# Down projection of four SwiGLU layers woven into their gate and up projection, nine 512-row pairs by seven products

## The chip, the cores and the metric

The kernel runs on one core of a Trainium2 chip. The metric is the device time of one execution in microseconds (us), lower is better; a measurement is a median of several executions, and the profile shows one execution with every instruction of the five engines: TensorE (PE, with its weight loads as PEld), VectorE (DVE), ScalarE (ACT), GpSimd (POOL) and SyncE (SP, which here only issues DMAs).

## The reference

Two layers of an encoder work on 256 tokens of width 1024, all in float32. Each layer has a half-step feed-forward block (below "FFN"), an attention block ("mix") and a second FFN:

```python
def swiglu(x, w_gate, w_up, w_down):
    return (jax.nn.silu(x @ w_gate) * (x @ w_up)) @ w_down

for l in range(DEPTH):
    x = x + 0.5 * swiglu(rms_norm(x, ffn1_norm[l]), ffn1_w_gate[l], ffn1_w_up[l], ffn1_w_down[l])
    ...
    x = x + merged @ w_out[l]
    x = x + 0.5 * swiglu(rms_norm(x, ffn2_norm[l]), ffn2_w_gate[l], ffn2_w_up[l], ffn2_w_down[l])
```

The inner width D_FF is 2816. Only the four FFNs and the way in which one block hands x to the next bear on this change; the attention is left as it is.

## The kernel before, in words

**Precision.** A float32 operand is split into a high part (rounded to the fast matmul type, on ScalarE) and a low part (the rest, on VectorE: `split_to`, L192 to L194). One product of two split operands is three matmuls, hi by hi, hi by lo, lo by hi (`three`, L176 to L179). So every weight tile of 128x1024 costs a DMA, one ACTIVATE and one TENSOR_TENSOR before TensorE can use it. The tiles come from rings: `raw` with 4 buffers, `wh` and `wl` with 6 each.

**One FFN** (`ffn`, L317) takes the inner width in 11 chunks of 256. For each chunk TensorE multiplies both token halves (t = 0 and 1, 128 tokens each) with the gate and up columns: `project`, 8 products of 128x512 for each half, 48 matmuls for a chunk. `glu` (L457) makes silu(gate) * up, `send` (L328) lays it out as 16-bit halves and starts a DMA transpose, and `arrive` (L337) puts the transposed chunk together and splits it. When all 11 chunks are through, `down` (L399) runs the down projection alone.

**The plan of the down projection** is a string of one letter for each chunk, `PLAN = "SFGFGGFGGSS"`. A chunk is two token halves by two 128-row blocks, against two rows by two column halves of w_down: eight products of blocks in the plain way ("S", `out_rows`). The other eight chunks use a seven-product scheme of fast 2x2 matrix multiplication: sums and differences of the four blocks of each side (`arrive` L348 to L350 for the activations, `differences` L366 for the weights), seven products "1" to "7" (`sevens`, L384), and at the end sums of the products (`combine`, L431). Here "1" means the block in the corner. Three of the eight chunks have their weight differences made ahead, during gate and up (`prepare`, PREP and PREP_FIRST), and read the rows of w_down once more for the rest.

**The end of a stage.** The last chunks are plain; after each group of products for a token half t and a column half d, VectorE adds the group to x (L311), and `norm` (L202) for the next stage is deferred by four products: TensorE transposes four blocks of x (L210), VectorE scales them by the gain (L217), ScalarE and VectorE split them, ScalarE sums the squares. The last FFN stores x instead.

**What sets the order.** The order of TensorE is that of the program. VectorE, ScalarE and SyncE are ordered by a scheduler; inside a tied chain (`linked`, L124, and `chain`) each instruction is made to follow the one before it on its engine in program order. Before the change only the opening of the first FFN is tied. All engines work through their own queues in order.

Of the kernel before, what the change touches and what calls it, by code (L numbers as in the profile page):

```python
# [2 lines left out]

# [12 lines left out]
U16 = mybir.dt.uint16  # L16
# [35 lines left out]
PLAN = "SFGFGGFGGSS"  # L52
PREP = {3: 1, 5: 3, 7: 6}
PREP_FIRST = {5: 1, 7: 3, 8: 6}
NS = sum(kind != "S" for kind in PLAN)
# [3 lines left out]
def hybrid_encoder(ctx, tc, x, w_gu1, w_d1, w_in, b_gate, qk_gain, rpb, sink, t5,  # L59
# [73 lines left out]
    def parts(r, nk=2, n=512):  # L133
        wh = ring.tile([P, 2, 512], F32R, name="wh", tag="wh", bufs=RING)
        wl = ring.tile([P, 2, 512], F32R, name="wl", tag="wl", bufs=RING)
        split_to(wh[:, :nk, :n], wl[:, :nk, :n], r)
        return wh, wl

    def load(src, nk, n):
        raw = ring.tile([P, 2, 512], F32, name="raw", tag="raw", bufs=RAW)  # L140
        r = raw[:, :nk, :n]
        nc.sync.dma_start(r, src)
        return parts(r, nk, n)
# [5 lines left out]
    def piece(w, l, i, c0, n, nk=KD // 2):  # L149
        at = (nk * c0 + i * n) * 2 * P  # L150
        return load(w[l, at:at + 2 * P * n].rearrange("(p k n) -> p k n", p=P, k=2), 2, n)
# [4 lines left out]
    def rows(w, l, k):  # L156
        return load(w[l, k * P:(k + 1) * P, :].rearrange("p (h n) -> p h n", h=2), 2, 512)
# [32 lines left out]
    last_hi = [None]  # L190

    def split_to(hi, lo, src):  # L192
        last_hi[0] = linked("act", lambda: nc.scalar.activation(hi, src, AF.Copy))  # L193
        linked("dve", lambda: nc.vector.tensor_tensor(lo, src, hi.bitcast(F32), ALU.subtract))  # L194
# [7 lines left out]
    def norm(t, n, half, apart=False):  # L202
# [9 lines left out]
        if apart and half == 1:  # L212
            for i in range(4):
                linked("act", lambda: nc.scalar.activation(xg[:, i, :], tp[:, i, :], AF.Copy,
                                                           scale=gain[:, n, 4 + i:5 + i]))
        else:
            linked("dve", lambda: nc.vector.tensor_tensor(  # L217
                xg, tp, gain[:, n, ks].unsqueeze(2).to_broadcast([P, 4, P]), ALU.mult))
        split_to(*(x[:, ks, :] for x in xT[t]), xg)
        if not apart:  # L220
            square(t, half)

# [73 lines left out]
    def out_rows(get, acc, k0, k1, last, w, l, scale, after, rest=None, split=None):  # L296
        pieces = [(k, *rows(w, l, k)) for k in range(k0, k1)]
        if split:
            split()
        for t in range(T):  # L300
            for d in range(2):
                for k, wh, wl in pieces:
                    first = acc[t][d] is None
                    if first:
                        acc[t][d] = out_bank(t, d)
                    xh, xl = get(t, k)
                    three(acc[t][d], xh, xl, wh[:, d, :], wl[:, d, :], first, last and k == k1 - 1)
                    tick(1)
                if last:
                    xd = xs[t][:, d * 512:(d + 1) * 512]  # L310
                    updated = nc.vector.scalar_tensor_tensor(xd, acc[t][d], scale, xd, op0=ALU.mult, op1=ALU.add)  # L311
                    if rest and t + d == 0:
                        with tc.issue_after(updated.ins):
                            rest()
                    after(t, d)

    def ffn(l, n, w_gu, w_d, after):  # L317
        with tc.tile_pool(name="ffn", bufs=1) as fp:
            hs = {}
            SLOT = ((1, 2), (0, 3))  # L320

            on_way, apart = [], {}

            def half(c, p, shape=None, dtype=F32R):
                m, n = (4, NFC - NS) if PLAN[c] == "S" else (7, NS)
                return fp.tile(shape or [P, m, P], dtype, name=p if shape else f"{p}{m}", tag=f"{p[:2]}{m}", bufs=n)

            def send(c, hh):  # L328
                m = 8 if PLAN[c] == "S" else 14
                z = half(c, "lo16", [P, m, P], U16)[:, :8, :].rearrange("p s n -> p (s n)")  # L330
                apart[c] = nc.scalar.activation(z.rearrange("p (two n) -> p two n", two=2),  # L331
                                                hh.bitcast(U16).rearrange("p s (n two) -> p two (s n)", two=2), AF.Copy)
                zT = half(c, "hi16", [P, m, P], U16)[:, :8, :]
                nc.sync.dma_start_transpose(zT, z)
                on_way.append((c, zT))

            def arrive():  # L337
                c, zT = on_way.pop(0)
                if PLAN[c] == "S":
                    a = fp.tile([P, 4, P], F32, name="a4", tag="a4")  # L340
                else:
                    a = fp.tile([P, 8, P], F32, name="a", tag="sums", bufs=2)
                joined = nc.scalar.activation(a[:, :4, :].bitcast(U16).rearrange("p s (n two) -> p two (s n)", two=2),  # L343
                                              zT.rearrange("p (two s) n -> p two (s n)", two=2), AF.Copy)
                behind(joined, apart[c + 1] if c + 1 < NFC else last_hi[0])
                hi, lo = half(c, "hi"), half(c, "lo")
                if PLAN[c] != "S":
                    for to, x, y, op in ((4, 0, 3, ALU.add), (6, 1, 0, ALU.subtract), (5, 4, 1, ALU.subtract),  # L348
                                         (7, 2, 5, ALU.subtract)):
                        nc.vector.tensor_tensor(a[:, to, :], a[:, x, :], a[:, y, :], op)  # L350
                    split_to(hi, lo, a[:, 1:, :])
                else:
                    split_to(hi, lo, a)
                hs[c] = (hi, lo)

            def get(t, k):
                return [h[:, SLOT[t][k % 2], :] for h in hs[k // 2]]

            stored = {}

            def block_row(k, c0=0, n=2):
                r = ring.tile([P, 2, 512], F32, name="raw", tag="raw", bufs=RAW)[:, :n, :]
                nc.sync.dma_start(r, w_d[l, k * P:(k + 1) * P, :n * 512].rearrange("p (h n) -> p h n", h=n))
                return r

            def differences(r0, r1, into):  # L366
                sub = lambda to, x, y: nc.vector.tensor_tensor(to, x, y, ALU.subtract)  # L367
                u = fp.tile([P, 2, 512], F32, name="u", tag="sums", bufs=2)
                sub(u[:, 0, :], r1[:, 1, :], r0[:, 1, :])
                sub(u[:, 1, :], r0[:, 1, :], r0[:, 0, :])  # L370
                us = into("u", u)
                v = fp.tile([P, 2, 512], F32, name="v", tag="sums", bufs=2)
                sub(v[:, 0, :], r1[:, 1, :], u[:, 1, :])
                sub(v[:, 1, :], r1[:, 0, :], v[:, 0, :])
                return us, into("v", v)

            def prepare(c):
                def into(name, r):
                    hl = [fp.tile([P, 2, 512], F32R, name=f"{name}{p}{c}", tag=f"{name}{p}{c}") for p in "hl"]
                    split_to(*hl, r)  # L380
                    return hl
                stored[c] = differences(block_row(2 * c), block_row(2 * c + 1), into)

            def sevens(c):  # L384
                r0 = block_row(2 * c, n=1 if c in stored else 2)
                r1 = block_row(2 * c + 1)
                place = ("xh0", "xl0", "xh1", "xl1")[(c - PLAN[:c].count("S")) % 4]
                both = act.tile([P, 2, 512], F32R, name="corner", tag=place)
                corner = [both[:, i, :] for i in range(2)]
                split_to(*corner, r0[:, 0, :])  # L390
                low = parts(r1)
                us, vs = stored.get(c) or differences(r0, r1, lambda name, r: parts(r))
                if on_way and c >= 5:
                    arrive()
                half = lambda pair, i: [p[:, i, :] for p in pair]
                return (("1", 0, corner), ("2", 1, half(low, 0)), ("3", 6, half(low, 1)), ("5", 3, half(us, 1)),
                        ("6", 4, half(vs, 0)), ("4", 2, half(vs, 1)), ("7", 5, half(us, 0)))

            def down():  # L399
                acc = [[None] * 2 for _ in range(T)]  # L400
                banks = {"2": (0, 0), "3": (0, 1), "4": (1, 0)}
                extra, rest = {}, []
                c = 0
                while c < NFC:
                    if PLAN[c] == "S":
# [460 lines left out]
```

## Time and profile before

| | |
|---|---|
| median of 3 runs | 1063.62 us (1062.95 to 1063.72) |
| the profiled execution | 1063.93 us, of which 1062.1 us are the span from its first to its last instruction |
| instructions | PE 4949, DVE 1337, ACT 1070, POOL 118 |
| first transposes of each next stage (L210) | 183.37, 352.74, 528.95, 706.16, 875.32 us |
| last matmul | 1057.83 us |
| data moved | 224.15 MB, mean 211 GB/s |

Split at those places, the span is six stages: FFN, mix, FFN, FFN, mix, FFN. The view of engine busy time by stretch shows them, with the columns: stretch, its length, busy time and instructions of PE, PEld, DVE, ACT and POOL, the granted TensorE clock, the share of DMA time, GB/s.

```profile
15.00:190.00 175.00, 172.22 (x752) 139.27 (x751) 146.88 (x203) 125.95 (x153) 17.80 (x27) 1.00 0.77 226
190.00:366.00 176.00, 175.84 (x936) 148.96 (x934) 146.11 (x269) 123.93 (x237) 48.67 (x40) 1.00 0.60 186
366.00:543.00 177.00, 176.91 (x787) 146.13 (x787) 150.22 (x204) 127.64 (x153) 1.11 (x2) 1.00 0.79 226
543.00:717.00 174.00, 173.23 (x771) 142.92 (x771) 146.93 (x201) 124.29 (x150) 1.10 (x2) 1.00 0.75 223
```

TensorE is busy nearly all of the time in every stage, VectorE for five sixths of it, ScalarE for seven tenths. The profile models the end of a matmul, so a stop of TensorE shows in full only from the start of one matmul to the start of the next.

### The profile page before, as it was taken

To read this page: it belongs to the slowest core of one execution; us is meant where nothing else is said; L and a number is where in the kernel's file an instruction comes from. 1 tells how busy PE (TensorE), PEld (TensorE's weight loads), DVE (VectorE), ACT (ScalarE), POOL (GpSimd) and SP (SyncE) were. 2 spreads that over 40 slices of the span, in tenths; PEclk is the share of its full clock that TensorE was granted. 3 is DMA by queue.
4 is the path that set the end of the run, shared out by engine and by line. 5 is a ranking of instruction groups with operands and counts; after the bars stand their busy time and mean duration, and the time that the engine had idled before them with its cause. 6 is when DMAs were issued, how large, how long until landed. Compare 5 with 4: busy or idle time off the path is not lost.

```text
span 1062.1 us, 14462 instructions
## 1 busy us (share of the span) xinstructions
PE 1052.2 (99%) x4949; PEld 871.4 (82%) x4949; DVE 878.6 (83%) x1337; ACT 747.6 (70%) x1070; POOL 118.6 (11%) x118
## 2 busy tenths in 40 slices
PE   9999999999999999999999999999999999999998
PEld 6888787888888888888888888878888888887886
DVE  6678899889886759879977887998898866788897
ACT  6777765788773667886567886757887646687772
POOL 1000040244420000000000000003534100000000
PEclk9999999999999999999999999999999999999999
DMA  7979866665655489996758997657566555798862
GB/s 247 262 225 254 253 207 200 204 193 176 194 182 159 159 231 259 258 252 196 228 171 224 275 262 202 214 160 249 174 198 177 189 159 189 214 277 227 240 201 99
DMA packets 112522, 224.15 MB, mean 211 GB/s; under 512 B 54032, under 2 KB 60208, under 8 KB 112448
## 3 DMA queue, kind: packets, MB, share of 16 engines
q1 hardware_dynamic: 112256, 223.14, 70.6%
q8 instruction: 39, 0.64, 0.2%
q0 software_dynamic: 192, 0.08, 0.1%
q14 instruction: 35, 0.29, 0.1%
HBM read 210.59 MB, written 1.06 MB: 199 GB/s over the span
## 4 chain that ended last, share of the span: by engine, by line
PE 76%; DVE 11%; DMA 6%; ACT 4%; issue 3%; SPq 0%; POOL 0%; ACTq 0%; DVEq 0%; POOLq 0%
PE g L177 18%; PE g L179 18%; PE g L178 18%; DVE wl L194 6%; DMA raw<-in_w_gu 4%; PE acc L177 4%; PE acc L179 4%; PE acc L178 4%; ACT wh L193 2%; DMA raw<-in_w_d 1%; PE sc L584 1%; PE po L619 1%; PE pt L605 1%; PE g L242 1%; ACT a L343 1%
## 5 line engine op out<-in xcount | busy, mean ns | idle before, releaser
L194 DVE TENSOR_TENSOR wl<-raw,wh 128x1024 fp32r<-128x1024 f32 x336 | 405.4, 1218 | 63.2 <-ACT wh L193 60.2
L193 ACT ACTIVATE wh<-raw 128x1024 fp32r<-128x1024 f32 x336 | 345.5, 1043 | 95.8 <-DMA raw<-in_w_gu 43.4
L177 PE MATMUL g<-wh,xh 128*128 128x512 f32 (+1 forms) x976 | 382.0, 391 | 0.6 <-DVE hh L463 0.3
L178 PE MATMUL g<-wl,xh 128*128 128x512 f32 (+1 forms) x976 | 377.7, 387 | 0.7 <-DVE wl L194 0.7
L179 PE MATMUL g<-wh,xl 128*128 128x512 f32 (+1 forms) x976 | 377.6, 387 | 0.1
L179 PEld LDWEIGHTS g<-wh,xl 128*128 128x128 f32 x976 | 183.4, 188 | 38.7 <-DVE xl L194 1.1
L177 PEld LDWEIGHTS g<-wh,xh 128*128 128x128 f32 x976 | 183.6, 188 | 35.9 <-DVE hh L463 2.4
L178 PEld LDWEIGHTS g<-wl,xh 128*128 128x128 f32 x976 | 183.7, 188 | 35.3 <-DVE wl L194 2.1
L178 PE MATMUL acc<-wl,hi 128*128 128x512 f32 x180 | 70.2, 390 | 1.3 <-DVE wl L194 1.3
L177 PE MATMUL acc<-wh,hi 128*128 128x512 f32 x180 | 70.8, 393 | 0.0
L179 PE MATMUL acc<-wh,lo 128*128 128x512 f32 x180 | 70.2, 390 | 0.0
L183 POOL TENSOR_TENSOR rs_y<-ms,mhalf 128x1 f32<-128x1 f32 x12 | 7.7, 644 | 542.6 <-DVE ms L231 533.8
L343 ACT ACTIVATE a<-hi 128x1024 uint16<-128x1024 uint16 x44 | 59.5, 1353 | 0.0
L463 DVE SCALAR_TENSOR_TENSOR hh<-g,rs_y,hh 128x256 f32<-128x256 f32 x88 | 42.1, 478 | 17.9 <-ACT hh L462 17.8
L331 ACT ACTIVATE lo<-hh 128x1024 uint16<-128x1024 uint16 x44 | 46.3, 1051 | 14.8 <-DVE hh L463 14.7
L462 ACT ACTIVATE hh<-g,rs_y 128x256 f32<-128x256 f32 x88 | 40.5, 461 | 22.2 <-PE g L179 21.7
L350 DVE TENSOR_TENSOR a<-a 128x128 f32<-128x128 f32 x128 | 31.9, 287 | 29.3 <-ACT a L343 28.6
L194 DVE TENSOR_TENSOR lo<-a,hi 128x896 fp32r<-128x896 f32 (+1 forms) x44 | 43.0, 977 | 11.1 <-ACT hi L193 11.1
L367 DVE TENSOR_TENSOR u<-raw 128x512 f32<-128x512 f32 x64 | 41.9, 684 | 11.8 <-DMA raw<-in_w_d 11.6
L597 POOL TENSOR_TENSOR S<-S,sm 128x512 f32<-128x512 f32 x32 | 37.1, 1159 | 65.5 <-DVE sm L596 34.6
L193 ACT ACTIVATE hi<-a 128x896 fp32r<-128x896 f32 (+1 forms) x44 | 37.7, 857 | 8.3 <-DVE a L350 7.8
L193 ACT ACTIVATE corner<-raw 128x512 fp32r<-128x512 f32 x32 | 20.0, 626 | 30.9 <-DMA raw<-in_w_d 26.0
(186 smaller groups left out, 1508.0 us busy)
## 6 DMA issues: line engine op xcount, KB each, us to landing
raw<-in_w_gu SPq DMA_DIRECT2D x176, 512.0 KB, 4.5
raw<-in_w_d SPq DMA_DIRECT2D x100, 512.0 KB, 4.3
raw<-in_w_in SPq DMA_DIRECT2D x64, 512.0 KB, 4.2
raw<-in_w_out SPq DMA_DIRECT2D x16, 512.0 KB, 3.5
bb<-in_b_gate SPq DMA_DIRECT2D x16, 256.0 KB, 3.4
raw<-in_w_bsw SPq DMA_DIRECT2D x8, 512.0 KB, 3.9
raw<-in_w_bna SPq DMA_DIRECT2D x8, 512.0 KB, 3.5
raw<-in_w_d SPq DMA_DIRECT2D x12, 256.0 KB, 2.7
```

Of the source, the lines that this page charges most:

```text
L177: nc.tensor.matmul(ps, xh, wh, start=first, stop=False)
L178: nc.tensor.matmul(ps, xh, wl, start=False, stop=False)
L179: nc.tensor.matmul(ps, xl, wh, start=False, stop=last)
L193: last_hi[0] = linked("act", lambda: nc.scalar.activation(hi, src, AF.Copy))
L194: linked("dve", lambda: nc.vector.tensor_tensor(lo, src, hi.bitcast(F32), ALU.subtract))
L331: apart[c] = nc.scalar.activation(z.rearrange("p (two n) -> p two n", two=2), hh.bitcast(U16).rearrange("p s (n two) -> p two (s n)", two= ...
L343: joined = nc.scalar.activation(a[:, :4, :].bitcast(U16).rearrange("p s (n two) -> p two (s n)", two=2), zT.rearrange("p (two s) n -> p tw ...
L350: nc.vector.tensor_tensor(a[:, to, :], a[:, x, :], a[:, y, :], op)
L367: sub = lambda to, x, y: nc.vector.tensor_tensor(to, x, y, ALU.subtract)
L462: linked("act", lambda: nc.scalar.activation(h, gate, AF.Silu, scale=rstd[t]))
L463: linked("dve", lambda: nc.vector.scalar_tensor_tensor(h, up, rstd[t], h, op0=ALU.mult, op1=ALU.mult))
L597: nc.gpsimd.tensor_tensor(S_, S_, sm.unsqueeze(2).to_broadcast([P, T, S]), ALU.mult)
```

## The change

The plan string, `prepare` and the separate phase `down` go. The first chunks of an FFN (three in the first FFN of the kernel, two in the others) run gate and up alone. From then on each pass of the loop does gate and up of chunk c and, behind it, six of the seven products of pair q = c - first_quad ("562374"); the seventh, "1", is kept for the end, with its operands in `one` and `corner`. Eight pairs (first FFN) or nine (the others) go by seven products, three or two chunks in the plain way at the end, with four column groups `plain`. The weight differences are made for each pair in the same pass from two rows of w_down held in a tile of their own (`rows`). From the second half of chunk first_quad - 1 on, all work of VectorE and ScalarE in an FFN is tied in program order. The stage end (`closing`) is tied too, also that of the attention block: each `norm` stands behind the next group of products, and two or three weight tiles of the next stage are loaded and split between its steps.

```diff
-PLAN = "SFGFGGFGGSS"
-PREP = {3: 1, 5: 3, 7: 6}
+HELD = 3
+SECOND_LAG = 4.0
+MIX_EARLY = 2
...
+    def start_split(hi, lo, src):
+        linked("act", lambda: nc.scalar.activation(hi, src, AF.Copy))
+        return lambda: linked("dve", lambda: nc.vector.tensor_tensor(lo, src, hi.bitcast(F32), ALU.subtract))
...
+    def closing(plain, n, early, between=lambda: None):
+        more = iter(early)
+        ahead = lambda: next(more, lambda: None)()
+        ahead()
+        plain(0, 1)
+        steps = norm_steps(0, n + 1, 0)
+        next(steps)
+        between()
+        next(steps)
+        plain(1, 0)
+        more_steps = norm_steps(0, n + 1, 1)
+        next(more_steps)
+        next(steps, None)
+        ahead()
+        next(more_steps)
+        plain(1, 1)
+        steps = norm_steps(1, n + 1, 0)
...
+        defer(SECOND_LAG, ("norm", 1, 1), lambda: norm(1, n + 1, 1))
+        chain.clear()
...
+            def quad(q, got):
+                for name in "562374":
+                    product(name, [h[:, SLOT[name], :] for h in hs[q]], got[name], q == QUADS - 1 and name in "567")
...
+            def down_end(rest, start):
+                p6, u = [act.tile([P, 512], F32, name=name, tag="xg", bufs=2) for name in ("p6", "ends")]
+                linked("act", lambda: nc.scalar.activation(p6, acc["6"], AF.Copy, scale=0.5))
...
+                for j in range(QUADS):
+                    product("1", [one[j][:, i, :] for i in range(2)], [corner[j][:, i, :] for i in range(2)],
+                            j == QUADS - 1)
...
+                plain(0, 0, "2")
+                if after:
...
+                closing(lambda t, d: plain(t, d, {(0, 1): "3", (1, 0): "4", (1, 1): "8"}[t, d]), n, early,
+                        lambda: linked("dve", lambda: nc.vector.tensor_tensor(x1, x1, twice(u), ALU.add)))
...
+                for j, (t, i) in enumerate(order):
+                    steps(ps, t, i, tiles[i])
+                    if j == 1:
+                        uv = sums(q)
+                        tile, low = start(c, 3)
+                        low()
+                        tiles.append(tile)
+                    elif j == 3:
+                        got.update(block("56", uv[:, :2, :]))
+                        got.update(block("23", rows_of[q][:, 2:, :]))
+                    elif j == 5:
+                        rest = arrive()
+                        got.update(block("74", uv[:, 2:, :]))
+                        rest()
+                        keep_corner(q)
+                ahead_tiles = []
+                tile, low = start(c + 1, 0)
+                ahead_tiles.append(tile)
+                steps(ps, 0, 3, tiles[3])
+                glu(0, ps[0], pair)
+                low()
+                tile, low = start(c + 1, 1)
+                ahead_tiles.append(tile)
+                steps(ps, 1, 3, tiles[3])
+                glu(1, ps[1], pair)
+                low()
+                tile, low = start(c + 1, 2)
+                ahead_tiles.append(tile)
+                send(c, pair[0])
+                low()
+                quad(q, got)
```

`steps(ps, t, i, tile)` is two products of gate and up for token half t; `sums` makes the four weight differences of a pair in three instructions, `block` splits two of them, `keep_corner` the corner block, `start` fetches a weight tile and starts its split. In `arrive` the corner block of the activations is split by itself (128x128) and the other six blocks in one go (128x768, before 128x896).

How this moves the instructions is seen on VectorE. The first place is the middle of the second FFN. Before, between one chunk's `glu` and the next, the rows are these (`wl` are low parts of gate and up weights, `u` and `v` weight differences made ahead, `a` the block sums of the activations, `hh` the glu):

```order
L463 SCALAR_TENSOR_TENSOR hh<-g,rs_y,hh 128x256
L194 TENSOR_TENSOR wl<-raw,wh 128x1024
L367 TENSOR_TENSOR v<-raw,u 128x512
L194 TENSOR_TENSOR wl<-raw,wh 128x1024
L367 TENSOR_TENSOR v<-raw,v 128x512
L194 TENSOR_TENSOR wl<-raw,wh 128x1024
L463 SCALAR_TENSOR_TENSOR hh<-g,rs_y,hh 128x2x128
```

Behind this stretch the same mixture goes on, and nothing of the products of a pair stands in it. In the changed kernel a pass of the same FFN reads, from the weight differences (`uv`, from the two `rows` of w_down) to the first `glu` and the low part behind it (`one` and `corner` are the operands of product "1"):

```order
L413 TENSOR_TENSOR uv<-rows 128x2x512
L413 TENSOR_TENSOR uv<-rows,uv 128x512 x2
L208 TENSOR_TENSOR wl<-raw,wh 128x1024
L208 TENSOR_TENSOR wl<-uv,wh 128x1024
L208 TENSOR_TENSOR wl<-rows,wh 128x1024
L208 TENSOR_TENSOR one_4089<-a,one_4089 128x128
L396 TENSOR_TENSOR a<-a 128x128 x4
L208 TENSOR_TENSOR wl<-uv,wh 128x1024
L208 TENSOR_TENSOR lo<-a,hi 128x768
L208 TENSOR_TENSOR corner_4104<-rows,corner_4104 128x512
L497 SCALAR_TENSOR_TENSOR hh<-g,rs_y,hh 128x256
L208 TENSOR_TENSOR wl<-raw,wh 128x1024
```

The second `hh` and two more `wl<-raw` close the pass. The work on a pair of w_down now stands inside the pass, in one fixed place, and three of the four `wl` of the next chunk stand around the two `hh`.

The second place is the end of the third FFN, VectorE again. Before, from the first addition of product sums to the second transposed half (`p` and `ends` are the sums of products, `x_80` and `x_81` the token halves of x, `acc` a plain group, `xg` the scaled transposed x):

```order
L437 SCALAR_TENSOR_TENSOR p_6725<-tp,p_6724 128x512 x2
L194 TENSOR_TENSOR wl<-raw,wh 128x1024
L311 SCALAR_TENSOR_TENSOR x_80<-acc,x_80 128x512
L437 SCALAR_TENSOR_TENSOR ends<-tp,p_6725 128x512
L442 TENSOR_TENSOR x_81<-x_81,p_6725 128x512
L442 TENSOR_TENSOR x_80<-x_80,p_6725 128x512
L442 TENSOR_TENSOR x_81<-x_81,ends 128x512
L217 TENSOR_TENSOR xg<-tp,x_80 128x512
```

Four instructions on product sums stand here between a plain group (`acc`) and the scaling of its transposes. In the changed kernel the same stretch (`m` are product sums, each in its own bank):

```order
L471 TENSOR_TENSOR x_80<-x_80,ends 128x512
L442 SCALAR_TENSOR_TENSOR x_80<-m_5599,x_80 128x512
L208 TENSOR_TENSOR wl<-raw,wh 128x1024
L442 SCALAR_TENSOR_TENSOR x_80<-m_5603,x_80 128x512
L234 TENSOR_TENSOR xg<-tp,x_80 128x512
L489 TENSOR_TENSOR x_81<-x_81,ends 128x1024
L208 TENSOR_TENSOR xl_6775<-xg,xh_6774 128x512
L442 SCALAR_TENSOR_TENSOR x_81<-m_5611,x_81 128x512
```

The additions for x_81 that stood between a group and its transposes are gone from there or stand behind them, and one weight tile of the next stage (`wl`) stands between the first group and the second.

More of the change, by code (lines that the diff above doesn't have):

```diff
@@ L317, in ffn @@
-    def ffn(l, n, w_gu, w_d, after):
-        with tc.tile_pool(name="ffn", bufs=1) as fp:
[L319 to L326, printed above, removed]
-            def send(c, hh):
[L329 to L333, printed above, removed]
+    def closing(plain, n, early, between=lambda: None):
[15 more added lines that the diff above has]
+        steps = norm_steps(1, n + 1, 0)
+        next(steps)
+        next(more_steps, None)
+        ahead()
+        next(steps)
+        next(steps, None)
+        defer(SECOND_LAG, ("norm", 1, 1), lambda: norm(1, n + 1, 1))
+        chain.clear()
@@ L338, in arrive @@
                 c, zT = on_way.pop(0)
[L339 to L397, printed above, removed]
@@ new lines, in ffn, with product @@
+            acc, used = {}, {}
+            def product(name, x, w, last):
+                if name not in acc:
+                    pool, tag, m = BANK[name]
+                    acc[name] = pool.tile([P, 512], F32, name=f"m{name}", tag=tag, bufs=m)
+                used[name] = used.get(name, 0) + 1
+                three(acc[name], *x, *w, used[name] == 1, last)
+                tick(1)
+            def quad(q, got):
+                for name in "562374":
+                    product(name, [h[:, SLOT[name], :] for h in hs[q]], got[name], q == QUADS - 1 and name in "567")
@@ L469, in ffn @@
                     both, second = opening(w_gu, l, lambda ps: glu(0, ps, pair))
-                elif n == 0 and c == 1:
-                    pieces = second
-                else:
-                    pieces = columns(w_gu, l, c * 512, 512)
-                if c >= 2:
-                    arrive()
-                prep = PREP if n else PREP_FIRST
-                if c in prep:
-                    prepare(prep[c])
-                for t in range(T):
-                    if not first:
-                        glu(t, project(t, pieces, 512), pair)
-                    elif t:
-                        glu(t, both[t], pair)
@@ new lines, in ffn @@
+                if c == first_quad - 1:
+                    fetch_rows(0)
+                    chain["act"], chain["dve"] = glu(0, project(0, pieces, 512), pair)
+                    tiles = []
+                    for i in range(3):
+                        tile, low = start(c + 1, i)
+                        low()
+                        tiles.append(tile)
+                    rest = arrive()
+                    glu(1, project(1, pieces, 512), pair)
+                    rest()
+                    send(c, pair[0])
+                    continue
@@ L488, in hybrid_encoder @@
+                send(c, pair[0])
+                low()
+                quad(q, got)
+                tiles = ahead_tiles
+            tile, low = start(NFC, 3)
+            low()
+            tiles.append(tile)
+            down_end(tiles, start)
+            chain.clear()
     vec_d = dram.tile([NH, 511], F32, name="vec_d")
```

289 lines of the change are left out of this document (190 added, 99 removed).

## The prediction

> **What bounds the kernel now.** I began with the busy times of the page:
>
> ```profile
> PE 1052.2 (99%) x4949; PEld 871.4 (82%) x4949; DVE 878.6 (83%) x1337; ACT 747.6 (70%) x1070; POOL 118.6 (11%) x118
> ```
>
> TensorE looks full, but the end of a matmul is modelled, so I asked the timeline of TensorE for the steps from start to start (columns: start, duration, instruction, idle before and what ended it). The first two rows have 13 matmuls between them, left out here:
>
> ```profile
> 107.63 0.39 PE L178 MATMUL g<-wl,xh 128*128 128x512 f32 x1
> ...
> 110.80 0.39 PE L177 MATMUL g<-wh,xh 128*128 128x512 f32 x1
> 111.39 0.50 PE L178 MATMUL g<-wl,xh 128*128 128x512 f32 x1 [0.20 <-DVE wl L194]
> 111.73 0.40 PE L179 MATMUL g<-wh,xl 128*128 128x512 f32 x1
> 111.96 0.39 PE L177 MATMUL g<-wh,xh 128*128 128x512 f32 x1
> ```
>
> Undisturbed, a 128x512 matmul takes (110.80 - 107.63) / 14 = 0.2264 us. The stop in the fourth row shows how a wait reads: the view says 0.20 us idle, but the step is 111.39 - 110.80 = 0.59, so 0.36 us are lost (0.20 plus 0.39 - 0.23 that the modelled end hides), and the next step, 0.34, loses 0.11 more. A wait of a matmul thus costs its idle time plus 0.27 us, one of a transpose its idle time plus 0.16.
>
> The Trainium skill ("Perfetto Trace Analysis", Identifying the Most-Contended Engine) holds matmul busy time a bad measure and goes by weight loads instead, 82% here. By it some 190 us would be left to win; but in the trace a stretch without a stop has the same share, so I read 82% as the full rate. That is this row of the busy times by stretch (PE, PEld, DVE, ACT, POOL busy, granted clock, DMA share, GB/s):
>
> ```profile
> 400.00:420.00 20.00, 20.00 (x90) 16.58 (x89) 17.77 (x27) 15.98 (x19) 0.00 (x0) 1.00 0.96 260
> ```
>
> 16.58 of 20 us are weight loads, TensorE never stops, and the clock is granted in full. So only two things can shorten this kernel: fewer matmuls, and the stops. All stops of TensorE that the waits view lists behind the opening are these (waiter, releaser: total idle us, times, longest):
>
> ```profile
> PE tp L210 <- DVE x L311: 1.5, 4, 0.6
> PE acc L178 <- DVE wl L194: 1.3, 1, 1.3
> PE g L178 <- DVE wl L194: 0.7, 2, 0.5
> PE g L177 <- DVE hh L463: 0.3, 1, 0.3
> PE pt L605 <- POOL S L597: 0.2, 1, 0.2
> ```
>
> **The change, part by part.**
>
> *Matmuls.* The plan string has eight seven-product letters and three plain ones, 8 x 7 + 3 x 8 = 80 products. Three of the four FFNs now have nine and two: 9 x 7 + 2 x 8 = 79. That is 3 products of 3 matmuls: 9 x 0.2264 = **2.0 us** on the path, since TensorE is the path.
>
> *Stops that go.* The first four rows above lie in or at the ends of FFNs, in code that is replaced: 1.5 + 1.3 + 0.7 + 0.3 = 3.8 us idle, plus 4 x 0.27 for the matmuls and 4 x 0.16 for the transposes, 5.5 us. Stops shorter than the modelled end show no idle time; two larger ones are
>
> ```profile
> 125.49 0.39 PE L179 MATMUL g<-wh,xl 128*128 128x512 f32 x1
> 125.98 0.50 PE L177 MATMUL g<-wh,xh 128*128 128x512 f32 x1
> ...
> 975.82 0.39 PE L179 MATMUL g<-wh,xl 128*128 128x512 f32 x1
> 976.32 0.50 PE L177 MATMUL g<-wh,xh 128*128 128x512 f32 x1
> ```
>
> of 0.49 and 0.50 us a step, so 0.26 + 0.27 lost and 0.11 twice behind them, 0.8 us. Together **6.3 us**. The row `pt` is in the attention and stays.
>
> *Does VectorE keep up in the woven pass?* TensorE needs 48 + 18 = 66 matmuls, 66 x 0.2264 = 14.94 us. For VectorE I take steps from start to start, since its instructions overlap:
>
> ```profile
> 428.30 1.22 DVE L194 TENSOR_TENSOR wl<-raw,wh 128x1024 fp32r<-128x1024 f32 x1 [0.34 <-ACT wh L193]
> 429.44 0.48 DVE L463 SCALAR_TENSOR_TENSOR hh<-g,rs_y,hh 128x256 f32<-128x256 f32 x1
> 429.83 1.21 DVE L194 TENSOR_TENSOR vl<-v,vh 128x1024 fp32r<-128x1024 f32 x1
> 430.97 1.22 DVE L194 TENSOR_TENSOR wl<-raw,wh 128x1024 fp32r<-128x1024 f32 x1
> ...
> 437.89 1.28 DVE L367 TENSOR_TENSOR u<-raw 128x512 f32<-128x512 f32 x2
> 440.36 1.02 DVE L350 TENSOR_TENSOR a<-a 128x128 f32<-128x128 f32 x4 [1.19 <-ACT a L343]
> ```
>
> A 128x1024 costs 1.14 (429.44 - 428.30), not 1.22, a `hh` 0.39, a 128x512 1.28 / 2 less the same overlap, 0.60, the four 128x128 together 1.0. A pass has eight 128x1024 (four `wl<-raw`, three of the pair, the double difference), 9.1; two `hh`, 0.8; two differences and the corner of 128x512, 1.8; the four sums, 1.0; the 128x128 part, 0.25 as a quarter of them; and a 128x768 that no row shows, between a 128x512 (0.60) and a 128x1024 (1.14), so 0.9. Sum **13.8 us**, 1.1 below TensorE's 14.94. ScalarE by the same reading:
>
> ```profile
> 428.52 1.06 ACT L193 ACTIVATE vh<-v 128x1024 fp32r<-128x1024 f32 x1
> 429.65 1.07 ACT L193 ACTIVATE wh<-raw 128x1024 fp32r<-128x1024 f32 x1
> 430.62 1.04 ACT L331 ACTIVATE lo<-hh 128x1024 uint16<-128x1024 uint16 x1
> 431.56 1.35 ACT L343 ACTIVATE a<-hi 128x1024 uint16<-128x1024 uint16 x1
> 432.79 0.45 ACT L462 ACTIVATE hh<-g,rs_y 128x256 f32<-128x256 f32 x1
> 433.13 1.05 ACT L193 ACTIVATE wh<-raw 128x1024 fp32r<-128x1024 f32 x1
> ```
>
> seven splits at 0.97, 6.8; the layout 0.94; the joining 1.23; two silus at 0.34, 0.7; the three smaller splits at most 0.97 each: 12.6 at most. Both fit, so the pass stays TensorE's.
>
> The Trainium skill ("VectorE: DVE Perf Modes", The DRAIN you can't avoid) says the next instruction doesn't start until the pipe is empty. By it each would cost its whole duration, and the pass over 15 us. The rows 429.44 and 429.83 speak against it: the second starts 0.09 us before the first has ended.
>
> *The tie.* Each `hh` now holds up everything behind it on VectorE, above all the `wl` of the next chunk. Following one pass from TensorE's first matmul: `steps(0, 3)` ends at 42 x 0.2264 = 9.5; ScalarE's silu (0.45) and `hh` (0.48) bring VectorE to 10.6, the first `wl` behind it to about 11.8. TensorE wants that tile at 14.94, 3 us later, the second and third 2.7 and 5.4 us after that. So VectorE may come late to `hh` by up to 3 us before TensorE stops, and each pass gives 1.1 us back. What is queued behind the waiting `hh` isn't late. I cost the tie at nothing; if that cover goes, the price is the excess of a pass over 14.94, 35 times.
>
> *Transfers.* SyncE's queue gets the two rows of a pair ahead of the last weight tile of a chunk and the transpose behind it. Landing, by the list of issues:
>
> ```profile
> raw<-in_w_gu SPq DMA_DIRECT2D x176, 512.0 KB, 4.5
> hi<-lo SPq DMA_TRANSPOSE x44, 4.3
> ```
>
> A pass moves six tiles of 512 KB in 14.94 us, about 210 GB/s, where the stretch from 400 us moved 260 without a stop of TensorE. A transpose lands 4.3 us after the layout; `arrive` wants it near two thirds of the next pass, and its sums feed the pair of the pass behind that. Behind the transpose in SyncE's queue stand three tiles that are wanted near the end of the next pass. Nothing for this either way.
>
> *Stage ends.* What happens there now, VectorE's timeline and then TensorE's:
>
> ```profile
> 180.36 2.35 DVE L194 TENSOR_TENSOR wl<-raw,wh 128x1024 fp32r<-128x1024 f32 x2
> 182.63 0.68 DVE L311 SCALAR_TENSOR_TENSOR x<-acc,x 128x512 f32<-128x512 f32 x1
> ...
> 183.37 0.66 PE L210 MATMUL tp<-ident,x 128*128 128x128 f32 x4 [0.56 <-DVE x L311]
> 183.78 0.48 PE L177 MATMUL acc<-wh,hi 128*128 128x512 f32 x1
> ```
>
> VectorE had weight tiles in front of the addition to x that the transposes need. In the new order only one tile stands there, and the transposes come a whole group (12 matmuls, 2.7 us) behind their addition, which takes 0.7. For each group VectorE then has an addition, a scaling, a low part (0.60 each) and a tile (1.14), 2.9 us, and once 1.14 for x_81; TensorE spends 2.7, and 0.4 for four transposes (183.37 to 183.78). Three groups, 9.9 against 9.4: VectorE ends half a microsecond late, and the first matmuls of the next stage use what was ready a group earlier. So I take no stop. The bounds for each of five tied ends are 0.1 below nothing (an unlisted stop that goes) and 1.2 us (what 183 costs today: 0.56 and 0.17 idle in two waits, 0.16 on each, rounded up).
>
> *Sum.* 1063.93 - 2.0 - 6.3 = 1055.6 for an execution like the profiled one. This stands 0.3 above the median of the runs, so **1055.3** for a median.
>
> **The rivals.**
>
> *A new wait at the stage ends.* The tied ends put tiles of the next stage between additions; if the old price of 1.2 us comes at two ends, the time is 1057.7, at all five 1061.3. For it: 9.9 against 9.4. Against it: the transposes have a group of margin.
>
> *VectorE at full duration.* If tied instructions no longer overlap, the 19 of a pass cost 13.8 + 19 x 0.08 = 15.3 against 14.94, 0.36 over in each of 35 passes, 13 us: 1068 if nothing catches it, 1056 with 3 us of margin in each of four FFNs; halfway is 1062, no change. Against it: the overlap stands in every back-to-back pair that I read. This is what the rule of the Trainium skill above would make of the change ("VectorE: DVE Perf Modes").
>
> *Hand-overs stop VectorE (slower).* In the tie it may not take another row when ScalarE isn't through:
>
> ```profile
> DVE wl L194 <- ACT wh L193: 61.4, 84, 4.4
> ```
>
> 0.73 us each. A pass has four places where VectorE needs ScalarE's fresh result of its own sums (first split of the pair, joined chunk, 128x768, corner). All four stopping cost 2.9, less 1.1 of slack, 1.8 x 35 = 63, less 12 us of margin: 1106; three, 1.1 x 35 - 12 = 26: 1081. It decides from 1.1 + (12 + 10.7) / 35 = 1.7 us idle a pass, more than two such stops. Against it: ScalarE has over 2 us to spare in a pass and can run ahead of all but these four.
>
> **How the numbers follow.** Forecast as worked out, with up to two stage ends at their price: 0.63, 1053.7 to 1057.7 (the low end is all five ends 0.1 better, `pt` gone with 0.4, and 0.7 allowed for stops too short for the view). Stage ends stopping more: 0.18, up to 1061.4. No change, at full duration or with stops merely swapped: 0.10. Slower: 0.09. A measurement here tells 0.2% from no change, 2.1 us; faster than 1061.5 is then 0.81, within 0.10, slower 0.09. The range reaches over the first rival, 1053.7 to 1061.0.
>
> **What would show it.** Right: about 66 matmuls in 15 us throughout a woven pass, `hh` of VectorE starting soon after its silu, no `tp` wait on x. Wrong: waits of TensorE on `wl` or `hh` that return every 15 us (the tie), on `tp`, `xl` or `wl` right behind the five stage borders (the ends), or VectorE rows with idle time behind ScalarE inside each pass.

## The result, and the profile after

The changed kernel takes 1054.87 us (median of 4 runs, 1054.08 to 1055.27); the kernel before, timed beside it, 1063.55 us (1062.95 to 1063.72). The ratio is 0.9918, 95% interval 0.9901 to 0.9936. Timed once more, beside 1066.32 us of the kernel before, it took 1054.28 us: 0.9889 (0.9872 to 0.9905). The forecast was 1055.3. The profiled execution is 1055.27 us long with a span of 1053.5.

The busy times of the page, after:

```profile
PE 1046.7 (99%) x4940; PEld 870.4 (83%) x4940; DVE 896.3 (85%) x1363; ACT 753.3 (72%) x1111; POOL 117.0 (11%) x118
```

Nine matmuls fewer, as counted, and more of VectorE's and ScalarE's time on a shorter span. The waits of TensorE (waiter, releaser: total us, times, longest) that the view lists are now these:

```profile
PE idle L121 <- DVE blank L116: 1.6, 1, 1.6
PE tp L227 <- DMA x<-in_x: 0.4, 1, 0.4
PE tp L637 <- DVE hv L622: 0.3, 1, 0.3
PE pt L714 <- POOL S L706: 0.3, 1, 0.3
PE g L194 <- DVE wl L208: 0.2, 1, 0.2
```

The first two are the opening. Of the four rows that the prediction wanted gone (`tp` on x, `acc` on `wl`, `g` on `wl`, `g` on `hh`) one remains with 0.2 us; `pt` stays, as it said. The row of `tp` L637 is new: it lies in the second attention block. Busy times by stretch, first from the second FFN, where 400 to 420 us was shown of before, then 14.94 us of a pass of the third FFN in which VectorE catches up:

```profile
400.00:420.00 20.00, 20.00 (x90) 16.57 (x89) 19.59 (x31) 16.58 (x22) 0.00 (x0) 1.00 0.63 194
567.33:582.27 14.94, 14.94 (x67) 12.38 (x66) 14.70 (x21) 12.29 (x16) 0.00 (x0) 1.00 0.77 240
```

TensorE never stops, although VectorE is busy 14.70 of the 14.94 us. (The 67th matmul only reaches into the stretch.) The last matmul of the kernel:

```profile
1049.20 0.39 PE L195 MATMUL m<-wh,lo 128*128 128x512 f32 x1
```

It began at 1057.83 before, so 8.63 us are won up to here. The table of first transposes of the next stage, before and after, shows where:

| first transposes of x for the next stage | before | after | won in the stretch | of it matmuls |
|---|---|---|---|---|
| 2nd stage end (first FFN and first attention) | 352.74 | 347.79 | 4.95 | 0 |
| 3rd (second FFN) | 528.95 | 523.17 | 0.83 | 3 |
| 4th (third FFN) | 706.16 | 698.56 | 1.82 | 3 |
| 5th (second attention) | 875.32 | 868.61 | -0.89 | 0 |
| last matmul (fourth FFN) | 1057.83 | 1049.20 | 1.92 | 3 |

Three matmuls are 0.68 us. The rest of each positive number is stops that went, less new ones. The stretch of the second attention is longer than before, although the last stop of a stage end (709.76 us before, 0.35 us lost) lies in it and went: the attention block itself lost 1.2 us.

### The profile page after: what moved, and what is told of

Same layout as the page of the kernel before. It is cut to its first block, busy times and chain, and to the rows that moved or that the text cites. A ratio compares the mean times of both kernels' runs of the same rounds, so it can differ in the third digit from the quotient of the medians.

```text
span 1053.5 us, 14250 instructions
## 1 busy us (share of the span) xinstructions
PE 1046.7 (99%) x4940; PEld 870.4 (83%) x4940; DVE 896.3 (85%) x1363; ACT 753.3 (72%) x1111; POOL 117.0 (11%) x118
## 4 chain that ended last, share of the span: by engine, by line
PE 93%; DVE 3%; DMA 1%; ACT 1%; issue 1%; POOL 0%; DVEq 0%; ACTq 0%; POOLq 0%
PE g L193 20%; PE g L194 20%; PE g L195 20%; PE m L195 7%; PE m L194 7%; PE m L193 7%; DVE wl L208 1%; PE po L728 1%; PE acc L193 1%; PE acc L194 1%; PE acc L195 1%; PE sc L693 1%; PE pt L714 1%; PE g L265 1%; PE tp L227 1%
## 5 line engine op out<-in xcount | busy, mean ns | idle before, releaser
L208 DVE TENSOR_TENSOR wl<-raw,wh 128x1024 fp32r<-128x1024 f32 (+1 forms) x296 | 354.6, 1217 | 37.6 <-ACT wh L207 37.1
L207 ACT ACTIVATE wh<-raw 128x1024 fp32r<-128x1024 f32 (+1 forms) x296 | 304.6, 1040 | 38.3 <-PE g L195 12.4
L207 ACT ACTIVATE wh<-uv 128x1024 fp32r<-128x1024 f32 x70 | 73.8, 1055 | 69.1 <-DVE uv L413 69.1
L193 PE MATMUL m<-wh,hi 128*128 128x512 f32 x274 | 107.2, 391 | 0.0
L195 PE MATMUL m<-wh,lo 128*128 128x512 f32 x274 | 106.7, 389 | 0.0
L194 PE MATMUL m<-wl,hi 128*128 128x512 f32 x274 | 106.7, 389 | 0.0
L208 DVE TENSOR_TENSOR wl<-uv,wh 128x1024 fp32r<-128x1024 f32 x70 | 85.5, 1222 | 1.0 <-ACT wh L207 1.0
L385 ACT ACTIVATE a<-zT 128x1024 uint16<-128x1024 uint16 x44 | 60.0, 1363 | 6.8 <-DMA zT<-z 6.7
L195 PEld LDWEIGHTS m<-wh,lo 128*128 128x128 f32 x274 | 51.4, 188 | 10.7
L194 PEld LDWEIGHTS m<-wl,hi 128*128 128x128 f32 x274 | 51.5, 188 | 10.5
```

Of the source, the lines that this page charges most:

```text
L193: nc.tensor.matmul(ps, xh, wh, start=first, stop=False)
L194: nc.tensor.matmul(ps, xh, wl, start=False, stop=False)
L195: nc.tensor.matmul(ps, xl, wh, start=False, stop=last)
L208: return lambda: linked("dve", lambda: nc.vector.tensor_tensor(lo, src, hi.bitcast(F32), ALU.subtract))
L385: linked("act", lambda: nc.scalar.activation(a[:, :4, :].bitcast(U16).rearrange("p s (n two) -> p two (s n)", two=2), zT.rearrange("p (two ...
```

## The experiments

Each is an edit of the changed kernel, so its ratio is to the kernel before, timed beside it, with the 95% interval.

### Take the tie away

```diff
-                    chain["act"], chain["dve"] = glu(0, project(0, pieces, 512), pair)
+                    glu(0, project(0, pieces, 512), pair)
...
-                chain["dve"] = linked("dve", lambda: nc.vector.scalar_tensor_tensor(xd, acc[t][d], scale, xd,
+                linked("dve", lambda: nc.vector.scalar_tensor_tensor(xd, acc[t][d], scale, xd,
```

> The woven kernel with nothing tied behind the opening: the scheduler orders VectorE and ScalarE in the passes and at the stage ends. Theory (the weave gives TensorE enough to do, and VectorE has 1.1 us to spare in each pass in any order): within 1 us of the woven kernel, 1054 to 1056. Rival (the fixed order is what keeps TensorE from stopping): stops come back in the passes and at the ends, 5 to 15 us slower, 1060 or more.

This unties the woven passes and all stage ends. Measured: 1081.15 us, 1.0166 (1.0125 to 1.0206). With the same matmuls and the same code of the woven pass, the kernel is slower than before. TensorE's waits, the first two rows:

```profile
PE g L193 <- DVE hh L497: 11.1, 12, 1.8
PE m L193 <- ACT hi L207: 5.8, 3, 2.5
```

One of those stops, by ScalarE's timeline ahead of it (start, duration, instruction, idle before and releaser), and then TensorE's row:

```profile
575.12 1.06 ACT L207 ACTIVATE wh<-uv 128x1024 fp32r<-128x1024 f32 x1 [0.52 <-PE g L195]
579.32 0.63 ACT L207 ACTIVATE corner<-rows 128x512 fp32r<-128x512 f32 x1 [3.14 <-DMA rows<-in_w_d]
579.86 1.04 ACT L207 ACTIVATE wh<-raw 128x1024 fp32r<-128x1024 f32 x1
580.81 1.36 ACT L385 ACTIVATE a<-zT 128x1024 uint16<-128x1024 uint16 x1
...
583.17 0.81 ACT L496 ACTIVATE hh<-g,rs_y 128x256 f32<-128x256 f32 x2
```

```profile
585.75 0.50 PE L193 MATMUL g<-wh,xh 128*128 128x512 f32 x1 [1.14 <-DVE hh L497]
```

ScalarE stands 3.14 us for rows of w_down, to split the corner that product "1" needs only at the end of the FFN. A weight tile, the joined chunk and both silus queue behind it, VectorE gets to `hh` at 585.21 by its timeline, and the matmul that needs the bank of that `hh` has been idle for 1.14 us. In this trace ScalarE stands 46.8 us (26 times) for rows of w_down and 63.4 us (32 times) for transposes; in the tied kernel the transposes cost it 6.7 us (5 times), and its waits list no rows of w_down. So it is the fixed order that keeps TensorE from stopping, and not the weaving by itself. What the fixed order alone would do for the kernel before, without the weaving, was not tested.

### Tie only one engine

```diff
+    free = [None]
+
     def linked(engine, emit):
+        if engine == free[0]:
+            return emit()
```

with `free[0]` set to one engine from the start of the weaving to the stage end.

> In the woven passes only VectorE is tied in program order; ScalarE's order there is the scheduler's again (the stage ends stay tied on both). Without any tie the time was 1081 us, and in its trace ScalarE stood for 63.4 us behind transposes that had not landed and 46.8 us behind rows of w_down, with silu queued behind. Theory (ScalarE's order is what makes the glu late): 1070 to 1081. Rival (VectorE's order is): 1054 to 1058.

> The other half: in the woven passes only ScalarE is tied, VectorE's order there is the scheduler's. Theory (ScalarE's order decides): 1054 to 1060. Rival (VectorE's order decides): 1065 to 1081. If each half alone repairs it or neither does, the two orders have to agree, and the tie counts as one thing.

Measured: ScalarE free 1115.28 us, 1.0467 (1.0447 to 1.0486); VectorE free 1073.4 us, 1.0073 (1.0057 to 1.009). Both theories of one deciding engine fall. With ScalarE free the time lies far above both ranges; with VectorE free it lies in the range of "VectorE's order decides", but by that reading ScalarE free would have been near 1055. Each half alone is slower than the kernel before, and tying VectorE alone is worse than no tie. VectorE's timeline with ScalarE free (lines are 3 or 4 higher here):

```profile
600.77 1.22 DVE L211 TENSOR_TENSOR wl<-rows,wh 128x1024 fp32r<-128x1024 f32 x1
603.30 0.29 DVE L211 TENSOR_TENSOR one<-a,one 128x128 fp32r<-128x128 f32 x1 [1.31 <-ACT one L210]
603.51 1.02 DVE L400 TENSOR_TENSOR a<-a 128x128 f32<-128x128 f32 x4
604.44 1.22 DVE L211 TENSOR_TENSOR wl<-uv,wh 128x1024 fp32r<-128x1024 f32 x1
608.17 0.96 DVE L211 TENSOR_TENSOR lo<-a,hi 128x768 fp32r<-128x768 f32 x1 [2.51 <-ACT hi L210]
609.05 0.68 DVE L211 TENSOR_TENSOR corner<-rows,corner 128x512 fp32r<-128x512 f32 x1
609.65 0.48 DVE L501 SCALAR_TENSOR_TENSOR hh<-g,rs_y,hh 128x256 f32<-128x256 f32 x1
```

ScalarE had both silus done by 606.45, but had put the split of the block sums behind them and a weight tile. VectorE, bound to its order, stands 2.51 us for that split with the ready `hh` behind it. Two such stops, 3.8 us, make this pass 17.9 us long. This is the mechanism of the rival "hand-overs stop VectorE", and it does end slower than before. With VectorE free the stop is the mirror image. VectorE's timeline in a pass, and ScalarE's largest wait (total us, times, longest):

```profile
601.77 1.22 DVE L417 TENSOR_TENSOR uv<-rows 128x1024 f32<-128x1024 f32 x1
602.91 0.69 DVE L211 TENSOR_TENSOR corner<-rows,corner 128x512 fp32r<-128x512 f32 x1
603.51 1.22 DVE L211 TENSOR_TENSOR wl<-raw,wh 128x1024 fp32r<-128x1024 f32 x1
604.64 0.48 DVE L501 SCALAR_TENSOR_TENSOR hh<-g,rs_y,hh 128x256 f32<-128x256 f32 x1
```

```profile
ACT z L379 <- DVE hh L501: 83.1, 38, 2.6
```

ScalarE ends the silu at 602.40, but VectorE does a weight difference, the corner and a weight tile before `hh`, and TensorE stops for that `hh` at 605.18 (0.84 us idle). ScalarE, bound to its order, stands 83.1 us for `hh` before it can lay it out (`z`); in the tied kernel that is 2.3 us in 3 waits. So the tie counts as one thing: the two engines need the same order, and need it together.

Long stops cost more than their idle time. With ScalarE free TensorE idles 2.34 us before 374.44 us, and a little later the granted clock falls to half:

```profile
375.70:379.10 3.40, 3.40 (x10) 2.63 (x9) 0.77 (x2) 2.86 (x4) 0.00 (x0) 0.50 1.03 416
```

In these 3.4 us a matmul takes 0.43 us instead of 0.227, some 1.6 us lost. The same happens four times in this run, twice in the untied one and once in the run with early transposes below, each time within 2 us behind a stop of 1.6 us or more; four other stops of 1.7 to 2.0 us brought none. The kernel before and the changed one have no such stretch before their last matmul.

### How much room VectorE has in a pass

```diff
-                                 (uv[:, 1, :], r[:, 3, :], uv[:, 0, :]), (uv[:, 3, :], r[:, 2, :], uv[:, 1, :])):
+                                 *[(uv[:, 1, :], r[:, 3, :], uv[:, 0, :])] * 2, (uv[:, 3, :], r[:, 2, :], uv[:, 1, :])):
```

and `* 4` for three more. The result is the same, VectorE's work grows.

> One more VectorE difference of 128x512 in each of the 35 woven passes (the same result written twice), 0.60 to 0.71 us each by the rows of the changed kernel. In its trace VectorE's first glu of a pass starts 12.0 us after the pass begins on TensorE, one pass on 11.2, then 10.4, then steadily 10.2: it gives back 0.8 a pass where the prediction said 1.1. Theory (a margin of 3 us, 0.8 a pass of spare): the addition fits, lateness shrinks by only 0.1 to 0.2 a pass, at most the first pass of an FFN stops TensorE by a few tenths: 1055 to 1057 us. Rival (VectorE bounds the woven pass already and every addition counts): 35 x 0.65 = 23 us more, 1078. Rival (VectorE has more spare than the trace shows): 1054.9, and the first glu still settles at 10.2 within three passes.

> Three more such differences in each pass, 1.8 to 2.1 us. By the prediction's ledger (1.1 spare a pass, 3 us of margin): 0.7 over in each pass, 35 x 0.7 = 25 less 4 x 3 = 12, 13 us more, 1068. By the trace of the changed kernel (0.8 spare, about 2.2 of the margin used up in the first pass): 1.1 over in each pass, 35 x 1.1 = 38 less about 4 x 1, 34 us more, 1089. If a wait for the operands of the pair ends first instead of VectorE, less than either.

Measured: one more, 1056.41 us, 0.9914 (0.9898 to 0.9931); three more, 1103.65 us, 1.036 (1.034 to 1.0379). A pass of the changed kernel on VectorE, from one pass's first difference to the next's:

```profile
569.73 1.22 DVE L413 TENSOR_TENSOR uv<-rows 128x1024 f32<-128x1024 f32 x1
570.98 1.42 DVE L413 TENSOR_TENSOR uv<-rows,uv 128x512 f32<-128x512 f32 x2
572.32 1.22 DVE L208 TENSOR_TENSOR wl<-raw,wh 128x1024 fp32r<-128x1024 f32 x1
573.46 1.22 DVE L208 TENSOR_TENSOR wl<-uv,wh 128x1024 fp32r<-128x1024 f32 x1
...
578.86 0.68 DVE L208 TENSOR_TENSOR corner<-rows,corner 128x512 fp32r<-128x512 f32 x1
579.68 0.48 DVE L497 SCALAR_TENSOR_TENSOR hh<-g,rs_y,hh 128x256 f32<-128x256 f32 x1
...
583.88 1.22 DVE L413 TENSOR_TENSOR uv<-rows 128x1024 f32<-128x1024 f32 x1
```

583.88 - 569.73 = 14.15 us, where the prediction had summed 13.8. Of the 0.35, 0.23 lies where an instruction reads the result of the one just ahead: 570.98 - 569.73 = 1.25 for a 1.22, where independent ones take 1.14 (573.46 - 572.32), and 0.73 for the first of the two differences, where the second takes 0.61. Another 0.2 lies in front of `hh` (579.68 - 578.86 = 0.82 for a 0.61): even in a pass that catches up it waits for the silu, which ScalarE ends at 579.65. The other rows take a little less than summed. TensorE takes 14.96 us from the first matmul of a pass to the first of the next, so VectorE gives back 0.8 each time. That can be watched: `hh` begins 12.0 us after the first matmul of its pass in the second pass of the second FFN, then 11.2, 10.4, 10.2, and stays there, since from then on VectorE stands 0.95 us a pass for the silu.

The time with one difference more is not told apart from the changed kernel. Its chain is 14.87 (0.72 us more, since the difference reads a fresh result too), and the start of `hh` shrinks only by 0.1 a pass, 13.2, 13.1, 13.0, 12.9; only the first pass of some FFNs stops TensorE, by up to 0.7 us. With three more it should be 14.15 + 3 x 0.72 = 16.31, and a pass of TensorE measures 16.33, with a stop on `wl` in each:

```profile
PE g L194 <- DVE wl L208: 22.5, 37, 1.0
```

So a pass costs the larger of 14.96 and VectorE's chain (with its one wait for the silu in it), and the room was 0.8 us. The expectation's own sums of 13 or 34 us for three were too small (48.8 over the first timing), because it priced a difference at 0.6 to 0.7 and let the margin absorb the excess once an FFN; by 1.37 us in each of 35 passes it is 48.

### Where the weaving begins

```diff
-        first_quad = 2 if n else 3
+        first_quad = 3
```

for eight pairs everywhere, `first_quad = 2` for nine everywhere.

> All four FFNs with eight pairs by seven products, woven and tied as before: 9 matmuls more. Theory (TensorE is the path): 9 x 0.2264 = 2.0 us slower than the woven kernel, and no new stop. Rival (the last chunks are easier in the plain way, with longer groups at the stage end): less than 1 us slower.

> Nine pairs in the first FFN as well: 3 matmuls fewer. Theory: 0.7 us faster, if the first pass finds its weights in time. Rival (the weaving would start while the opening's transfers are still late): stops of TensorE between 26 and 60 us cost more than 0.7 us.

Measured: eight pairs 1056.9 us, 0.992 (0.9899 to 0.994); nine in the first FFN too 1058.45 us, 0.9932 (0.9914 to 0.995). The profiled execution with eight pairs, 1058.56 us, lies 3.3 above the changed kernel's: nine matmuls, 2.0, and 1.2 of stops near 27 and 60 us. Those stops are not the edit's: they lie in the first FFN, whose program the edit leaves as it is, and they differ between executions of the same kernel (the changed kernel loses 0.44 us at 58 us in its first profile and nothing there in its second). The medians lie 2.0 apart, as the theory has it, but the ratios hardly differ (0.992 against 0.9918 and 0.9889), and their intervals reach 2 us to either side. So the count of matmuls says what the ninth pair is worth, and the time does not contradict it. Nine pairs in the first FFN save three matmuls and lose more at its start: three stops there, 3.2 us idle. ScalarE's timeline, and then the matmul that waits:

```profile
34.43 1.36 ACT L385 ACTIVATE a<-zT 128x1024 uint16<-128x1024 uint16 x1 [4.68 <-DMA zT<-z]
35.82 0.31 ACT L207 ACTIVATE one<-a 128x128 fp32r<-128x128 f32 x1
36.04 0.46 ACT L496 ACTIVATE hh<-g,rs_y 128x256 f32<-128x256 f32 x1
...
37.84 0.50 PE L193 MATMUL g<-wh,xh 128*128 128x512 f32 x1 [2.04 <-DVE hh L497]
```

The joined chunk stands in tied order ahead of the silu, and its transpose took 8.32 us to land (26.09 to 34.41, by the chain of waits) where the median of this run is 4.2. In these 8.32 us the DMA engines were full with the first weights (a share of 1.05 by the busy times by stretch, 307 GB/s). A tie makes a late transfer everyone's.

### The stage ends

The tie off from the start of `closing` (at the three FFN ends; at the ends of the two attention blocks the first addition to x sets the chain anew, so the tie comes back there), then the tie on but each transposed half directly behind its own group of products:

```diff
     def closing(plain, n, early, between=lambda: None):
+        chain.clear()
```

```diff
         ahead()
-        plain(0, 1)
         steps = norm_steps(0, n + 1, 0)
         next(steps)
         between()
         next(steps)
-        plain(1, 0)
-        more_steps = norm_steps(0, n + 1, 1)
-        next(more_steps)
         next(steps, None)
+        plain(0, 1)
...
```

> Tied passes, but the five stage ends are left to the scheduler. Theory (the old stops at the stage ends came from weight tiles that the scheduler put ahead of the additions to x): the waits of the transposes on x come back, 1 to 3 us. Rival (they went because the transposes stand a whole group later): no change, no wait of a transpose on x.

> At the five stage ends each transposed half stands directly behind its own group of products again and not one group (12 matmuls, 2.7 us) later; the order on VectorE and the ties stay otherwise. Theory (the distance of a group is what took the stops at the ends away): each of the three transposes of an end waits for the last matmul of its group (0.39) and the addition to x (0.69), less the 0.23 of a matmul's step, 0.85 to 1.1 us; 15 of them, 13 to 16 us more: 1068 to 1071, with a wait of tp on x in the view of waits. Rival (the tie or the single weight tile on VectorE took them away): 1055 to 1057, no such wait.

Measured: without the tie 1054.23 us, 0.9894 (0.9877 to 0.9912), no wait of `tp` on x; it is not told apart from the changed kernel (0.9918 and 0.9889). With the transposes early 1077.45 us, 1.0108 (1.0093 to 1.0123), and these waits of TensorE, with one of the stops below:

```profile
PE tp L227 <- DVE x L357: 9.4, 8, 2.0
PE tp L227 <- DVE x L442: 8.2, 10, 1.1
```

```profile
531.64 0.66 PE L227 MATMUL tp<-ident,x 128*128 128x128 f32 x4 [0.79 <-DVE x L442]
```

Such a step loses 0.95 us (0.79 and 0.16), as expected, in 13 of the 18 waits; three of the other five are on the fourth half of an end, which is pressed too, and the two longest idle 2.0 us. The distance of a group is thus worth some 22 us. But it is not what the change brought: the kernel before deferred its `norm` by four products, the same distance. There four stops remained at two ends, since VectorE did weight tiles and product sums ahead of the addition. Both were FFN ends, where the run without the tie has no such stop. Neither the tie (off, no stop) nor the distance (the same) explains that they went. What is left is the other placing of those sums and tiles in the program; no run tested that alone, so it stays argued.

### Smaller edits, and a repeat

```diff
-NORM_LAG, QK_LAG, P_LAG, V_LAG, M_LAG = 4.0, 16, 10, 7.5, 5.5
+NORM_LAG, QK_LAG, P_LAG, V_LAG, M_LAG = 4.0, 18, 10, 7.5, 5.5
```

> The transposes of normed queries and keys in both attention blocks come two products later (16 to 18). The changed kernel's trace has new stops of 0.51 and 0.26 us at 730.8 and 733.3 us, in the second attention block, on rows of these tiles. Theory (they are a matter of that lag): both go, 0.6 us less, 1054.2, and nothing else moves. Rival (the lag of 16 is a compromise and the heads behind start later): the transposes of attention heads stop TensorE instead, 1055 to 1058.

1056.4 us, 0.9909 (0.9892 to 0.9925): inside the rival's range, though not told apart from the changed kernel. The stop at 730.8 goes (it all but goes in the repeat without an edit too, see below) and a longer one comes in each attention block (1.3 us idle in both), on the keys that the transposes feed; the second:

```profile
741.37 0.51 PE L693 MATMUL sc<-skT,sqT 128*128 128x256 f32 x2 [0.86 <-DVE skT L657]
```

The version without ties at the ends, with one head's transposes a product later:

```diff
-MORE = {"Q1": 2, ("sw", 4): 1.5, ("na", 4): 2, ("na", 5): 1.5}
+MORE = {"Q1": 2, ("sw", 4): 1.5, ("na", 3): 1, ("na", 4): 2, ("na", 5): 1.5}
```

> The version without ties at the stage ends, and one product more before the transposes of the fourth head of the second kind in each attention block, which waits for GpSimd in every trace (0.2 to 0.3 us idle, a step of 0.42). Expected from the version without these ties (1054.2 where this kernel was 1054.9): 0.3 us less in each of two blocks at most, 1053.7. Rival (that head's tiles are wanted later on): the next heads stop TensorE by as much, 1054.2 to 1055. Either is near what five rounds can tell.

1053.81 us, 0.9887 (0.9873 to 0.9902). The `pt` wait is gone from its trace. The last run, the changed kernel without an edit, shows whether that beats it:

> The changed kernel itself, without an edit, beside the kernel before. In the later runs the kernel before read 1065.3 to 1066.3 where it had read 1063.6 beside the changed kernel's first timing. Theory (the kernel before has stops that vary with the execution, the changed one hardly): 1055 again, a ratio of 0.989 to 0.991. Rival (these chips run everything 0.2% slower): 1057, a ratio of 0.992 as first measured. It also says how far the version without ties at the stage ends and with the later head (0.9887, 0.9873 to 0.9902) stands from the changed kernel.

1054.28 us, 0.9889 (0.9872 to 0.9905). It does not measurably beat it. It also shows that the medians of the kernel before differ more between timings (1063.55 to 1066.32) than those of the changed one (1054.28 and 1054.87); why was not looked into.

## Why the prediction was right

- **The bound.** TensorE at 0.2264 us a matmul without a stop was the right reading: where nothing waits, the changed kernel runs at the same step, and all that was won is matmuls and stops.
- **Matmuls, 2.0 us.** 4949 to 4940; right.
- **Stops, 6.3 us.** 8.63 - 2.04 = 6.6 us net. The stops that the prediction listed lost 6.28 us by TensorE's steps from start to start, as priced, and none of them is left. That the net is so near is luck. Some 1.9 us of smaller stops went too (0.5 at 145 and 159 us, 0.4 at 542 us, 0.25 in the opening, the rest 0.2 or less each), and 1.6 us came: 0.44 at 58 us and 1.2 in the second attention block. No term foresaw either, and they nearly cancel. This is the largest of the new ones, of transposes of normed queries:

```profile
730.83 0.85 PE L637 MATMUL tp<-ident_r,qs 128*128 128x128 f32 x8 [0.34 <-DVE hv L622]
```

  Such stops in the attention blocks differ from execution to execution, though. In the repeat of the same kernel this row is gone from the waits, and another is longer:

```profile
PE pt L714 <- POOL S L706: 1.2, 2, 0.9
```

- **VectorE keeps up.** Right, with less room: 14.15 us for 13.8, 0.8 spare for 1.1. By the law of the runs with more work, two such differences more (15.6 us) would cost 0.6 in each pass, some 22 us, and the change would be slower than before; no run had two.
- **The tie at nothing.** Right, and its argument (late `hh` by up to 3 us, given back pass by pass) is what the trace shows: 1.8 us late in the second pass of an FFN, then 0.8 less each pass. What it did not see is that the tie is what makes the weaving pay at all: untied, the same program is 1.7% slower than before.
- **Transfers at nothing.** Right in the steady passes, where ScalarE's waits for transposes are 6.7 us and reach TensorE nowhere. The run with nine pairs in the first FFN shows the place where it would have been wrong.
- **Stage ends without a stop.** Right in result; the margin of a group that it named is real (22 us without it), but the kernel before had it too.
- **The rivals.** Full duration on VectorE did not come: independent instructions overlap by 0.08 in the tied pass too. Where the next one reads the fresh result they don't (1.25 us from start to start at a duration of 1.22). The prediction gave half of what the Trainium skill says there ("VectorE: DVE Perf Modes", The DRAIN you can't avoid): the same paragraph adds that a next instruction that is not held starts earlier. The independent ones here do, by 0.08 us. The slower rival, hand-overs that stop VectorE, is real: in the changed kernel one is left in a pass, 0.14 us idle in front of `hh`, and with ScalarE's order free it came in full.

## What to carry to other kernels

In this kernel the woven loop stayed free of stops as long as VectorE's chain, summed from start to start and with dependent neighbours at full duration, was below TensorE's pass; an excess counted in every pass, and no margin absorbed it. Fix the order on all engines that hand results to each other: fixing VectorE's alone was worse here than fixing nothing. In a fixed order, put what waits for a transfer behind what TensorE waits for, and do not begin such a loop while the transfers are still saturated.

## What the runs showed of the hardware

- VectorE's successive 128x1024 instructions start 1.14 us apart at a duration of 1.22 when independent, and 1.25 when the second reads what the first wrote (569.73 and 570.98).
- A transpose by DMA took 8.3 us to land instead of the median 4.2 while the DMA engines were full (a share of 1.05, 307 GB/s).
- Behind a stop of TensorE of 1.6 us or more the granted clock fell to 0.50 for 3.4 us in seven places of three runs, and a matmul of 128x512 took 0.43 us instead of 0.227. Four other stops of 1.7 to 2.0 us brought no such fall.
- VectorE at 98% of a stretch (14.70 of 14.94 us) left TensorE without a stop, and so did one more instruction of 128x512 in a pass, but for the first pass of some FFNs; three more turned the same engine into the bound.
